# Accumulator loads moved to the front of each product, with their buffers swapped, and one GpSimd instruction taken off the root of a norm

## The chip, the cores and the metric

The kernel runs on one core of a Trainium2 chip. The metric is the device time of one execution in microseconds (us); lower is better. Most executions of one kernel agree within 0.3%.

## What is computed

The reference is one hybrid decoder block on x of 1024 rows by 1024 columns, in float32. Only its second half is touched here:

```python
x = x + jnp.einsum('bse,ed->bsd', mix, w_out[l])          # mix: retention and attention heads
h2 = rms_norm(x, norm2_g[l])
ff = jax.nn.silu(jnp.einsum('bsd,df->bsf', h2, w_gate[l])) * jnp.einsum('bsd,df->bsf', h2, w_up[l])
x = x + jnp.einsum('bsf,fd->bsd', ff, w_down[l])
```

`rms_norm` divides each row by the root of its mean square plus 1e-6. The hidden width D_FF is 2816.

## The kernel before

Every float32 product is made of three matmuls on rounded parts (`mm3`): each operand is split into a high part (a cast on ScalarE, tiles `whi` or the first half of `act`) and a low part (a subtraction on VectorE, tiles `wlo` or the second half of `act`). The three matmuls are high by high, high by low, low by high, so the second one needs the low part of the right operand.

The rows are eight tiles t of 128. The columns are two halves of 512, q or dh. Two stages matter.

**The middle stage** (`mid`, with `MID_PLAN`) computes `x2 = x + mix @ w_out` tile by tile on TensorE, and beside it the second norm. The plan is a list of (step, operation, arguments), and the engines keep its order. For a tile t: `o_add` adds x (VectorE) and stores the half to DRAM as `x2d`; `n_square` squares a half on ScalarE and sums each row into a column of the small tile `sso`; `n_rs` (lines 1024 to 1029) turns the two sums into the inverse root on GpSimd, with three instructions: add the two columns, times 1/D plus EPS, power of -0.5; `n_scale` multiplies each half of x2 by that root and the gain on VectorE, in place; `n_turn` transposes it on TensorE into a PSUM bank `h`; `n_back`, `n_hi`, `n_lo`, `f_sum` and so on make the operands of a Strassen product out of it. GpSimd also holds the first weight sums of the gate (`gw_sum`, tile `sum` from `rawp`).

**The gate and up stage** computes the hidden activations in eleven column groups of 256. In each, the four gate results are tiles of the pool `rowb`, the four up results tiles of the pool `rowa` (both named `c`; each pool has eight buffers), and VectorE multiplies up by gate. The results, and five sums of them (`plane`, tile `fsum`, made on GpSimd), are stored to DRAM as `ffd`.

**The last stage** multiplies by w_down, as seven Strassen products n of eleven steps c each (lines 1294 to 1320). In step c the left operand is loaded from `ffd` into a ring of eight slots (`a_load`, eight steps ahead), the right operand comes from w_down (`w_get`) and is where needed summed on GpSimd (`sum` from `wide`); both are split (`operand`); then twelve matmuls of 128x512 follow. At the end of a product the four PSUM banks are added on VectorE into `acc` tiles. There are sixteen of these; each begins as a piece of `x2d`, loaded by a DMA at line 1311, and the pieces that the first three products need are listed in `STARTS`. The last column group's five `fsum` planes are made inside the first product, at the steps of `LAST`.

All of these loads and stores are issued from one queue, that of SyncE (SP), which takes them in order: one that waits holds back all behind it. A scheduler sets the final order on the queue and on GpSimd.

Of the kernel before, what the change touches and what calls it, by code (L numbers as in the profile page):

```python
# [10 lines left out]
F32 = mybir.dt.float32  # L11
F32R = mybir.dt.float32r
AF = mybir.ActivationFunctionType
ALU = mybir.AluOpType
AX = mybir.AxisListType

P = 128
S = 1024
D = 1024
# [7 lines left out]
EPS = 1e-6  # L27
# [306 lines left out]
def block_kernel(ctx: ExitStack, tc: tile.TileContext, x, norm1_g, w_in, ret_norm_g, dq_g, dk_g,  # L334
# [17 lines left out]
    V, A, G, T = Pinned(nc.vector), Pinned(nc.scalar), Pinned(nc.gpsimd), Pinned(nc.tensor)  # L352
# [7 lines left out]
    rowa = ctx.enter_context(tc.tile_pool(name="rowa", bufs=NT))  # L360
# [15 lines left out]
    def bankp():  # L376
        return psum.tile([P, 512], F32, tag="pp", name="pp")

    def mm3(o, ah, al, bh, bl, first, last):
        T.matmul(o, ah, bh, start=first, stop=False)  # L380
        T.matmul(o, ah, bl, start=False, stop=False)
        T.matmul(o, al, bh, start=False, stop=last)

    def rsqrt(dst, src, n):

        G.tensor_tensor(out=dst, in0=src, in1=nhalf[:, :n], op=ALU.pow)

    def bankm(shape):
        return psum.tile(shape, F32, tag="m", name="m")
# [499 lines left out]
    x2 = [[None, None] for _ in range(NT)]  # L889
# [58 lines left out]
    for s in range(ND + NR + 3):  # L948
# [13 lines left out]
        if s == ND + 3:  # L962
            dif.close()
            rowb = ctx.enter_context(tc.tile_pool(name="rowb", bufs=NT))
# [11 lines left out]
        t = s - ND - NR  # L976
# [14 lines left out]
    NH = NF // 2  # L991
# [4 lines left out]
    def bankh():  # L996
        return hps.tile([P, 512], F32, tag="h", name="h")
# [17 lines left out]
    sums = {}  # L1015

    def n_square(t, i):

        if t not in sums:
            sums[t] = st.tile([P, 2], F32, name="sso", bufs=4)  # L1020
        sq = ap.tile([P, 512], F32, tag="sq", name="sq", bufs=1)
        A.activation(sq, x2[t][i], AF.Square, accum_out=sums[t][:, i:i + 1])

    def n_rs(t):

        ss2 = sums[t]
        G.tensor_tensor(out=ss2[:, 0:1], in0=ss2[:, 0:1], in1=ss2[:, 1:2], op=ALU.add)
        G.tensor_scalar(ss2[:, 1:2], ss2[:, 0:1], 1.0 / D, EPS, op0=ALU.mult, op1=ALU.add)
        rsqrt(ss2[:, 0:1], ss2[:, 1:2], 1)

    def n_scale(t, q):
        h2[t] = x2[t]
# [178 lines left out]
    for at, f, *args in MID_PLAN:  # L1211
        if at > step:
# [4 lines left out]
    DOWN = [(((1, 1), None, None), ((1, 0), (0, 0), ALU.subtract), {(0, 0): 1, (1, 0): 1}, ()),  # L1217
            (((1, 0), (1, 1), ALU.add), ((0, 0), None, None), {(1, 0): 1, (1, 1): -1}, ((1, 0),)),
            (((1, 0), (0, 0), ALU.subtract), ((0, 1), (0, 0), ALU.add), {(1, 1): 1}, ()),
            (((0, 0), (1, 1), ALU.add), ((1, 1), (0, 0), ALU.add), {(0, 0): 1, (1, 1): 1}, ()),  # L1220
            (((0, 0), (0, 1), ALU.add), ((1, 1), None, None), {(0, 0): -1, (0, 1): 1}, ()),
            (((0, 0), None, None), ((0, 1), (1, 1), ALU.subtract), {(0, 1): 1, (1, 1): 1}, ((0, 1), (1, 1))),
            (((0, 1), (1, 1), ALU.subtract), ((1, 0), (1, 1), ALU.add), {(0, 0): 1}, ((0, 0),))]
# [12 lines left out]
    acc = [[None, None] for _ in range(NT)]  # L1236
    at = {}

    def w_get(c, j, dh):

        if (c, j, dh) not in at:
            f = 2 * c + j
            to = at[c, j, dh] = kept[len(at)]
            nc.sync.dma_start(to, w_down[0, f * P:(f + 1) * P, dh * 512:(dh + 1) * 512])
        return at[c, j, dh]

    def a_load(i):

        nc.sync.dma_start(ring[i % len(ring)], ffd[i // NH, i % NH])

    def plane(n, c):
        a0, a1, aop = DOWN[n][0]
        src = up[a0[1], a0[0]]
        if a1 is not None:
            both = ap.tile([P, 512], F32, tag="sum", name="fsum", bufs=2)
            G.tensor_tensor(out=both, in0=src, in1=up[a1[1], a1[0]], op=aop)
            src = both
        nc.sync.dma_start(ffd[n, c], src)
# [23 lines left out]
    def operand(x_, y_=None, op=None):  # L1282
        hi, lo = (wp.tile([P, 512], F32R, tag=tag_, name=tag_) for tag_ in ("whi", "wlo"))
        if y_ is not None:
            both = wp.tile([P, 512], F32, tag="raw", name="sum", bufs=NRAW)
            G.tensor_tensor(out=both, in0=x_, in1=y_, op=op)
            x_ = both
        A.copy(hi, x_)
        V.tensor_tensor(out=lo, in0=x_, in1=hi.bitcast(F32), op=ALU.subtract)
        return hi, lo  # L1290

    STARTS = [((0, 0), (1, 0)), ((1, 1),), ((0, 1),)]
    LAST = {3 + i: n for i, n in enumerate(n for n in range(7) if DOWN[n][0][1] is not None)}
    for n, (_, (b0, b1, bop), outs, done) in enumerate(DOWN):
        m = [bankh() for _ in range(4)] if n % 2 == 0 else [bankp(), bankp(), bankm([P, 512]), bankm([P, 512])]
        for c in range(NH):
            b = [w_get(c, *name) for name in (b0, b1) if name is not None]
            i = n * NH + c
            ah, al = operand(ring[i % len(ring)])
            if i + len(ring) < 7 * NH:  # L1300
                a_load(i + len(ring))
            bh, bl = operand(*b, bop) if bop else operand(*b)
            if i in LAST:
                plane(LAST[i], NH - 1)

            if n < len(STARTS) and c >= NH - 4:
                t0 = c - NH + 4
                for sh, dh in STARTS[n]:
                    t = 4 * sh + t0
                    acc[t][dh] = (rowb if dh else rowa).tile([P, 512], F32, tag="rowb" if dh else "rowa", name="acc")  # L1310
                    nc.sync.dma_start(acc[t][dh], x2d[t * P:(t + 1) * P, dh * 512:(dh + 1) * 512])
            for t in range(4):
                mm3(m[t], ah[:, t * P:(t + 1) * P], al[:, t * P:(t + 1) * P], bh, bl, c == 0, c == NH - 1)
        for t in range(4):
            for (sh, dh), sign in outs.items():
                o = acc[4 * sh + t][dh]
                V.tensor_tensor(out=o, in0=o, in1=m[t], op=ALU.add if sign > 0 else ALU.subtract)
                if (sh, dh) in done:
                    row = (4 * sh + t) * P
                    nc.sync.dma_start(out[0, row:row + P, dh * 512:(dh + 1) * 512], o)  # L1320
# [25 lines left out]
```

## Time and profile before

| | |
|---|---|
| median of 3 runs | 1228.01 us (1226.68 to 1230.36) |
| the profiled execution | 1226.93 us, of which the span from first to last instruction is 1225.1 us |
| TensorE busy | 1204.8 us (98%) |
| VectorE, GpSimd, ScalarE busy | 838.1, 570.8, 537.2 us |
| middle stage, TensorE | about 500 to 609 us from the span's start |
| last stage, TensorE | 1007 to 1219 us |
| granted TensorE clock, mean | 0.996 |

Rows of the timeline read: start, duration (both us), engine, line, operation, output and inputs, and how many instructions are merged; in brackets how long the engine sat idle before, and what ended that. PE is TensorE, DVE VectorE, ACT ScalarE, POOL GpSimd. Nearly all rows have line 347, that of a helper which issues every instruction, so that groups are told apart by tile names.

### The profile page before, as it was taken

Reading aid. Unit: us, or ns where it says so; the run is one execution under the profiler, and the core shown is the slowest. Engines: PE = TensorE matmul, PEld = TensorE weight load, DVE = VectorE, ACT = ScalarE, POOL = GpSimd, SP = SyncE. Lnnn points to the kernel's source line nnn. Section 1 sums busy time; section 2 is a strip of 40 time slices with the busy share of each in tenths; the row PEclk is TensorE's granted clock in tenths of the full one; section 3 lists DMA queues with packets and bytes.
Section 4 is the critical chain, followed back from the end, with each engine's and each line's share of the span. In section 5 each row is a group of like instructions: output and inputs, shape, how many; then the busy total and the mean of one; then the engine's idle time right before and its main releaser. Section 6 shows DMA issues by size and latency. Waiting matters only on the chain. (4 is left out here: it accounts for less than half of the span.)

```text
span 1225.1 us, 17316 instructions
## 1 busy us (share of the span) xinstructions
PE 1204.8 (98%) x5944; PEld 1020.6 (83%) x5944; DVE 838.1 (68%) x1491; ACT 537.2 (44%) x1194; POOL 570.8 (47%) x719
## 2 busy tenths in 40 slices
PE   8999999999999999999899999999999999999998
PEld 7898989888888888787688888888888888788887
DVE  6988888854444445545997665757657659698697
ACT  6856666643222224434544344333443434344442
POOL 2656555644444443102276456545566536154053
PEclk9999999999999999999999999999999999999999
DMA  6201011102111111422233333323334177943342
GB/s 201 67 21 32 27 30 35 44 17 88 52 35 40 39 35 45 154 84 72 60 122 119 95 103 112 128 71 103 104 112 129 69 254 247 349 144 99 95 116 83
DMA packets 97383, 117.34 MB, mean 96 GB/s; under 512 B 8976, under 2 KB 60304, under 8 KB 97296
## 3 DMA queue, kind: packets, MB, share of 16 engines
q1 hardware_dynamic: 95968, 115.65, 29.5%
q8 instruction: 47, 0.77, 0.3%
q10 hardware_dynamic: 1328, 0.60, 0.3%
q14 instruction: 40, 0.33, 0.1%
HBM read 87.64 MB, written 28.57 MB: 95 GB/s over the span
## 5 line engine op out<-in xcount | busy, mean ns | idle before, releaser
L347 PE MATMUL pp<-whi,act 128*128 128x384 f32 (+1 forms) x896 | 287.8, 373 | 0.7 <-ACT whi L347 0.7
L347 POOL TENSOR_TENSOR sum<-rawp 128x512 f32<-128x512 f32 x110 | 157.2, 1430 | 174.5 <-DVE wlo L347 152.6
L347 ACT CAST whi<-sum 128x512 fp32r<-128x512 f32 x165 | 102.6, 622 | 204.9 <-PE h L347 62.8
L347 DVE TENSOR_TENSOR wlo<-sum,whi 128x512 fp32r<-128x512 f32 x165 | 167.7, 1016 | 34.0 <-ACT whi L347 33.5
L347 PE MATMUL h<-act,whi 128*128 128x512 f32 x608 | 187.5, 389 | 0.3 <-DVE act L347 0.3
L347 PEld LDWEIGHTS pp<-whi,act 128*128 128x128 f32 x896 | 167.4, 189 | 15.2 <-ACT whi L347 1.0
L347 PE MATMUL pp<-wlo,act 128*128 128x384 f32 (+1 forms) x448 | 161.6, 361 | 0.6 <-DVE wlo L347 0.6
L347 POOL TENSOR_TENSOR sum<-wide 128x512 f32<-128x512 f32 x55 | 85.7, 1560 | 134.0 <-DVE wlo L347 101.9
L347 PEld LDWEIGHTS h<-act,whi 128*128 128x128 f32 x608 | 114.1, 188 | 24.5 <-DVE act L347 0.7
L347 PE MATMUL pp<-wrh,act 128*128 128x512 f32 x384 | 130.7, 402 | 0.0
L347 PE MATMUL h<-act,wlo 128*128 128x512 f32 x304 | 118.3, 389 | 0.0
L347 DVE TENSOR_TENSOR wlo<-wide,whi 128x512 fp32r<-128x512 f32 x99 | 78.5, 816 | 32.5 <-ACT whi L347 32.5
L347 PE MATMUL m<-act,whi 128*128 128x512 f32 x312 | 97.7, 394 | 1.8 <-ACT act L347 1.2
L347 ACT CAST whi<-wide 128x512 fp32r<-128x512 f32 x99 | 59.3, 620 | 87.3 <-PE m L347 48.0
L347 PE MATMUL pp<-act,whi 128*128 128x512 f32 x312 | 96.4, 390 | 0.7 <-DVE act L347 0.7
L347 PEld LDWEIGHTS pp<-wlo,act 128*128 128x128 f32 x448 | 85.1, 190 | 7.6 <-DVE wlo L347 1.2
L347 POOL TENSOR_TENSOR fsum<-c 128x512 f32<-128x512 f32 x55 | 79.2, 1451 | 11.0 <-DMA ffd<-fsum 11.0
L347 PEld LDWEIGHTS pp<-wrh,act 128*128 128x128 f32 x384 | 72.2, 188 | 14.3
L347 DVE TENSOR_TENSOR c<-c,h 128x512 f32<-128x512 f32 x88 | 58.1, 682 | 32.6 <-PE h L347 32.5
L347 DVE TENSOR_TENSOR wlo<-rawp,whi 128x512 fp32r<-128x512 f32 x44 | 47.4, 1077 | 41.1 <-ACT whi L347 40.2
L347 PE MATMUL pp<-wrl,act 128*128 128x512 f32 x192 | 74.8, 390 | 0.0
L347 PEld LDWEIGHTS m<-act,whi 128*128 128x128 f32 x312 | 59.2, 190 | 14.6 <-ACT act L347 1.4
(162 smaller groups left out, 2515.7 us busy)
## 6 DMA issues: line engine op xcount, KB each, us to landing
wide<-ffd SPq DMA_DIRECT2D x77, 256.0 KB, 2.7
ffd<-fsum SPq DMA_DIRECT2D x55, 256.0 KB, 2.0
rawp<-in_w_gate_dram SPq DMA_DIRECT2D x22, 512.0 KB, 3.8
rawp<-in_w_up_dram SPq DMA_DIRECT2D x22, 512.0 KB, 3.9
wide<-in_w_down_dram SPq DMA_DIRECT2D x44, 256.0 KB, 5.3
raw<-in_w_in_dram SPq DMA_DIRECT2D x32, 256.0 KB, 2.8
ffd<-c SPq DMA_DIRECT2D x22, 256.0 KB, 2.0
raw<-in_w_in_dram SPq DMA_DIRECT2D x26, 192.0 KB, 2.5
```

Of the source, the lines that this page charges most:

```text
L347: i = getattr(self.engine, op)(*args, **kw)
```

## The change

The root: ScalarE's square now scales its input by D to the power of -0.5, so that the sums come out as means. After a tile's first square, a GpSimd instruction adds EPS to that column at once. `n_rs` then has two instructions, the add of the columns and the power. So there are still three per tile, but one of them stands earlier.

The accumulators: a product n of the first three loads its `acc` pieces at its steps 0 to 3 and no longer at steps 7 to 10, and the pieces with dh = 0 now lie in `rowb`, those with dh = 1 in `rowa`. The steps of `LAST` move from 3 to 7 to 4 to 8.

```diff
-        A.activation(sq, x2[t][i], AF.Square, accum_out=sums[t][:, i:i + 1])
+        A.activation(sq, x2[t][i], AF.Square, scale=D ** -0.5, accum_out=sums[t][:, i:i + 1])
+
+        if t not in eased:
+            eased.add(t)
+            G.tensor_scalar(sums[t][:, i:i + 1], sums[t][:, i:i + 1], EPS, None, op0=ALU.add)
+
+    eased = set()
...
         G.tensor_tensor(out=ss2[:, 0:1], in0=ss2[:, 0:1], in1=ss2[:, 1:2], op=ALU.add)
-        G.tensor_scalar(ss2[:, 1:2], ss2[:, 0:1], 1.0 / D, EPS, op0=ALU.mult, op1=ALU.add)
-        rsqrt(ss2[:, 0:1], ss2[:, 1:2], 1)
+        rsqrt(ss2[:, 0:1], ss2[:, 0:1], 1)
...
-    LAST = {3 + i: n for i, n in enumerate(n for n in range(7) if DOWN[n][0][1] is not None)}
+    LAST = {4 + i: n for i, n in enumerate(n for n in range(7) if DOWN[n][0][1] is not None)}
...
-            if n < len(STARTS) and c >= NH - 4:
-                t0 = c - NH + 4
+            if n < len(STARTS) and c < 4:
                 for sh, dh in STARTS[n]:
-                    t = 4 * sh + t0
-                    acc[t][dh] = (rowb if dh else rowa).tile([P, 512], F32, tag="rowb" if dh else "rowa", name="acc")
+                    t = 4 * sh + c
+                    acc[t][dh] = (rowa if dh else rowb).tile([P, 512], F32, tag="rowa" if dh else "rowb", name="acc")
                     nc.sync.dma_start(acc[t][dh], x2d[t * P:(t + 1) * P, dh * 512:(dh + 1) * 512])
```

The order on TensorE, VectorE and ScalarE is the same as before. On SP's queue, these rows follow the last of the loads of w_down for the first product (`ffd<-c` and `ffd<-fsum` are stores of the last column group, `wide<-ffd` are ring loads). Before:

```order
L1258 DMA ffd<-c 128x512 x2
L1249 DMA wide<-ffd 128x512 x4
L1258 DMA ffd<-fsum 128x512
L1249 DMA wide<-ffd 128x512
L1258 DMA ffd<-fsum 128x512
L1249 DMA wide<-ffd 128x512
L1258 DMA ffd<-fsum 128x512
L1249 DMA wide<-ffd 128x512
L1258 DMA ffd<-fsum 128x512
L1249 DMA wide<-ffd 128x512
L1258 DMA ffd<-fsum 128x512
L1311 DMA acc<-x2d 128x512 x2
```

At the same place after the change (its lines stand four or five further down in the file):

```order
L1263 DMA ffd<-c 128x512 x2
L1254 DMA wide<-ffd 128x512 x3
L1315 DMA acc<-x2d 128x512 x2
L1254 DMA wide<-ffd 128x512
L1315 DMA acc<-x2d 128x512 x2
L1254 DMA wide<-ffd 128x512
L1263 DMA ffd<-fsum 128x512
L1254 DMA wide<-ffd 128x512
L1263 DMA ffd<-fsum 128x512
L1254 DMA wide<-ffd 128x512
L1263 DMA ffd<-fsum 128x512
L1254 DMA wide<-ffd 128x512
```

Before, the eight pieces for the first product's sums begin behind the fifth store of an `fsum`. Now the first four of them go out in the gate and up stage's last group (where four pieces for the second product stood), and the other four stand here, ahead of the first store of an `fsum`. The pieces for the second and third product now follow behind the fifth store.

On GpSimd, around the roots of tiles 5, 6 and 7 (`sso_6756`, `sso_6850`, `sso_6953`), with the gate's weight sums between them. Before:

```order
L347 TENSOR_TENSOR sso_6756<-sso_6756 128x1
L347 TENSOR_SCALAR sso_6756<-sso_6756 128x1
L347 TENSOR_TENSOR sso_6756<-sso_6756,cs_77 128x1
L347 TENSOR_TENSOR sum_6880<-rawp_6405,rawp_6407 128x512
L347 TENSOR_TENSOR sso_6850<-sso_6850 128x1
L347 TENSOR_SCALAR sso_6850<-sso_6850 128x1
L347 TENSOR_TENSOR sso_6850<-sso_6850,cs_77 128x1
L347 TENSOR_TENSOR sum_6932<-rawp_6405,rawp_6407 128x512
```

After:

```order
L347 TENSOR_TENSOR sso_6756<-sso_6756 128x1
L347 TENSOR_TENSOR sso_6756<-sso_6756,cs_77 128x1
L347 TENSOR_SCALAR sso_6850<-sso_6850 128x1
L347 TENSOR_TENSOR sum_6881<-rawp_6408,rawp_6410 128x512
L347 TENSOR_TENSOR sso_6850<-sso_6850 128x1
L347 TENSOR_TENSOR sso_6850<-sso_6850,cs_77 128x1
L347 TENSOR_TENSOR sum_6932<-rawp_6408,rawp_6410 128x512
L347 TENSOR_SCALAR sso_6953<-sso_6953 128x1
```

The instruction between add and power is gone, and the one that adds EPS for tile 6 now stands ahead of the gate's first weight sum, where it waits for the first square of tile 6. That of tile 7 stands behind the second weight sum.

## Prediction

> **What bounds the kernel now.** I read the page first, then the waits of TensorE, then the timelines where it waited.
>
> ```profile
> span 1225.1 us, 17316 instructions
> ```
>
> The execution took 1226.93 us, so 1.8 us lie around this span. It is 1.08 us below the median of the runs, 1228.01; the sum is made against the execution and then moved up by that. TensorE is busy 98% of the span, so only time in which it stands still, or runs slowly, can be won. Stretches of the span by engine show where (busy us and instructions of PE, PEld, DVE, ACT, POOL, then granted clock, DMA share, GB/s):
>
> ```profile
> 505.00:605.00 100.00, 94.08 (x432) 75.65 (x431) 62.03 (x87) 42.54 (x86) 18.53 (x31) 0.98 0.28 92
> ...
> 1037.00:1067.00 30.00, 27.11 (x113) 21.94 (x112) 19.05 (x28) 10.99 (x20) 4.42 (x3) 0.94 0.98 345
> ```
>
> TensorE lacks 5.9 of 100 us in the one and 2.9 of 30 in the other, and the granted clock is below 1.00 in both. The change touches both: the roots lie in the first, the moved loads' sums in the second. Who made TensorE wait (total us, times, longest):
>
> ```profile
> PE pp L347 <- DVE wlo L347: 4.0, 4, 2.9
> PE h L347 <- DVE x L347: 3.2, 4, 1.2
> ```
>
> The longest single wait is 2.9 us for a low part `wlo`. TensorE there, at the beginning of the second product's third step:
>
> ```profile
> 1042.38 0.39 PE L347 MATMUL pp<-whi 128*128 128x512 f32 x1
> 1045.65 0.50 PE L347 MATMUL pp<-wlo,whi 128*128 128x512 f32 x1 [2.89 <-DVE wlo L347]
> ...
> 1047.55 0.63 PE L347 MATMUL m<-whi,wlo 128*128 128x512 f32 x1
> 1047.98 0.63 PE L347 MATMUL m<-whi 128*128 128x512 f32 x1
> ...
> 1050.54 0.42 PE L347 MATMUL pp<-whi 128*128 128x512 f32 x1
> ...
> 1051.03 0.39 PE L347 MATMUL pp<-whi,wlo 128*128 128x512 f32 x1
> ```
>
> And the chain that ended last gives the full pace, six matmuls in 1.36 us, 0.227 each:
>
> ```profile
> 1052.78 1.36 PE pp L347 x6
> ```
>
> From 1042.38 to 1051.03 there are 17 matmuls: 8.65 us where full pace takes 3.85. So 4.80 us are lost: 1045.65 - 1042.38 - 0.23 = 3.04 standing still, and 1.76 because from about 1047.2 to 1050.5 the starts lie 0.43 apart, half pace. The half pace begins 1.5 us behind the stop and ends by itself after 3.4; I count it with the stop.
>
> VectorE at the same time explains the stop:
>
> ```profile
> 1032.89 3.09 DVE L347 TENSOR_TENSOR wlo<-wide,whi 128x512 fp32r<-128x512 f32 x5
> 1036.41 0.69 DVE L347 TENSOR_TENSOR acc<-acc,h 128x512 f32<-128x512 f32 x1 [0.44 <-PE h L347]
> 1037.71 0.69 DVE L347 TENSOR_TENSOR acc<-acc,h 128x512 f32<-128x512 f32 x1 [0.61 <-DMA acc<-x2d]
> ...
> 1043.71 1.28 DVE L347 TENSOR_TENSOR acc<-acc,h 128x512 f32<-128x512 f32 x2 [0.69 <-DMA acc<-x2d]
> 1044.91 7.68 DVE L347 TENSOR_TENSOR wlo<-wide,whi 128x512 fp32r<-128x512 f32 x9
> ```
>
> Five splits end at 1035.98. Then eight adds of the first product stand ahead of the split that TensorE wants. The last two adds start at 1043.71 and take 0.60 each until the next instruction; eight would take 4.8. But they take from 1036.41 to 1044.91, 8.5, because most of them wait for their piece of `x2d`. SP's queue says why the pieces are late:
>
> ```profile
> 1012.51 0.80 SPq L1258 DMA_DIRECT2D ffd<-c  x2
> 1013.41 4.05 SPq L1249 DMA_DIRECT2D wide<-ffd  x4
> ...
> 1032.82 0.92 SPq L1311 DMA_DIRECT2D acc<-x2d  x2
> ```
>
> ```profile
> DMA to landing us min/median/max: 2.0/3.5/6.8
> ```
>
> The first two leave at 1032.82, and landing takes 3.5 in the median, up to 6.8. (The first add's 0.44 is put down to TensorE; 1032.82 + 3.5 = 1036.3 says it was the load.)
>
> **Part 1: the accumulators' loads.** Four of the eight pieces now leave in the gate stage, the other four behind three ring loads that follow the `ffd<-c` stores of 1012.51. Their slots in `rowb` are the last gate tiles, which VectorE's multiplications free before that very store can leave. The four ring loads at 1013.41 took 4.05 with their waits, so I put the last of the pieces at about 1019 and, at the longest landing, in place by 1026, 10 us ahead of the first add. The adds then run from 1035.98 at 0.60 each to 1040.8. The split behind them needs 0.74 (1044.91 to TensorE's 1045.65), so it is there at 1041.5; TensorE asks at 1042.61. Margin 1.1. The whole 3.04 goes, and with the stop its 1.76: **4.80 us**.
>
> What is late next? On SP's queue, ring loads and `fsum` stores now stand behind four more pieces: about 2 us later at 1017, where the ring is eight steps of 2.7 (twelve matmuls) ahead of TensorE. Behind the fifth store, eight pieces for later sums are mixed with loads of w_down, which the third product needs, nine steps or 24 us after the stop; DMA is busy 0.98 of that stretch, but four loads fewer fall into it. On GpSimd the third `fsum` moves behind the last weight sum, and the fifth must wait for the third's store; the number of its instructions ahead of the adds is the same. If one or two of them fall beside VectorE's splits that ran alone before, each costs VectorE about 1.0 (a scaling below takes 1.77 beside a GpSimd sum and 0.75 alone): with one the margin is used up, with two about 1 us of the stop stays. Bounds: 3.8 to 4.8.
>
> **Part 2: the root.** TensorE waits for a scaled tile four times. Tile 0 waits for something else: its second scaling follows the store of that half, which must have been read out before it is overwritten.
>
> ```profile
> 510.70 0.75 DVE L347 SCALAR_TENSOR_TENSOR x<-x,sso,gtile 128x512 f32<-128x512 f32 x1 [2.07 <-DMA x2d<-x]
> ```
>
> That gives nothing. Tile 5:
>
> ```profile
> 556.26 0.19 POOL L347 TENSOR_TENSOR sso<-sso 128x1 f32<-128x1 f32 x1 [10.71 <-ACT sq L347]
> ...
> 556.54 0.19 POOL L347 TENSOR_SCALAR sso<-sso 128x1 f32<-128x1 f32 x1
> ...
> 556.82 0.54 POOL L347 TENSOR_TENSOR sso<-sso,cs 128x1 f32<-128x1 f32 x1
> ...
> 557.33 1.29 POOL L347 TENSOR_TENSOR sum<-rawp 128x512 f32<-128x512 f32 x1
> 557.40 2.43 DVE L347 SCALAR_TENSOR_TENSOR x<-x,sso,gtile 128x512 f32<-128x512 f32 x2 [1.37 <-POOL sso L347]
> ...
> 559.31 0.63 PE L347 MATMUL h<-cs,x 128*128 128x128 f32 x4 [0.59 <-DVE x L347]
> ```
>
> From one GpSimd instruction to the next are 0.28, so without the middle one the power ends 0.28 earlier. More happens behind it. The weight sum at 557.33 ran beside the first scaling, and the scalings differ by whether one does:
>
> ```profile
> L347 DVE SCALAR_TENSOR_TENSOR x<-x,sso,gtile x16: 739/749/1772, 507.9 to 585.8; 128x512 f32<-128x512 f32 x16
> ```
>
> The median is 0.75, the longest 1.77. Now the sum stands behind the EPS instruction of tile 6, which waits for that tile's first square:
>
> ```profile
> 563.67 0.19 ACT L347 ACTIVATION_READ_ACCUMULATOR sq<-x 128x1 f32 x1
> ...
> 568.67 0.60 ACT L347 CAST whi<-sum 128x512 fp32r<-128x512 f32 x1
> ...
> 570.44 1.77 DVE L347 SCALAR_TENSOR_TENSOR x<-x,sso,gtile 128x512 f32<-128x512 f32 x1 [0.44 <-POOL sso L347]
> ...
> 572.36 0.63 PE L347 MATMUL h<-cs,x 128*128 128x128 f32 x4 [0.38 <-DVE x L347]
> ```
>
> The square's sum is there at 563.9, so the weight sum runs at about 564.2 to 565.5, and its cast is not due before 568.67. The first scaling of tile 5 then takes 0.75: 1.0 + 0.28 earlier, more than the 0.59 that TensorE waits. I take **0.59**. By the start alone (0.28) the term would be 0.28. [...]
>
> Tile 6 (the last two rows): TensorE idles 0.38; the power starts 0.28 earlier, and the scaling, 1.77 here, may get ahead of the weight sum. I take **0.38** (0.2 to 0.38). Tile 7:
>
> ```profile
> 581.35 0.58 POOL L347 TENSOR_TENSOR sso<-sso 128x1 f32<-128x1 f32 x1 [0.63 <-ACT sq L347]
> ...
> 582.01 0.51 POOL L347 TENSOR_SCALAR sso<-sso 128x1 f32<-128x1 f32 x1
> ...
> 582.61 0.55 POOL L347 TENSOR_TENSOR sso<-sso,cs 128x1 f32<-128x1 f32 x1
> ...
> 583.20 0.75 DVE L347 SCALAR_TENSOR_TENSOR x<-x,sso,gtile 128x512 f32<-128x512 f32 x1 [0.72 <-POOL sso L347]
> ...
> 586.69 0.63 PE L347 MATMUL h<-cs,x 128*128 128x128 f32 x4 [1.06 <-DVE x L347]
> ...
> 589.61 0.68 PE L347 MATMUL m<-act,whi 128*128 128x512 f32 x1 [0.63 <-DVE act L347]
> ...
> 593.59 0.40 PE L347 MATMUL m<-act,wlo 128*128 128x512 f32 x1
> ```
>
> Here a small GpSimd instruction takes 0.60, and VectorE's scaling waits for it with 0.72 idle. The 0.60 pass on to the transposes at 586.69 (1.06 idle) and in part to the low part at 589.61, which has sums and splits between them: **0.5** (0.36 to 0.60). The EPS instructions add 0.28 each where GpSimd otherwise waits for the square; the square itself keeps its shape and gets a constant factor, for which I take 0. The largest they could cost is 8 x 0.28 = 2.2 if each stood on the path, and none does.
>
> From 589.61 to 593.59 TensorE starts ten matmuls: 3.98 us where full pace takes 2.27, again about half pace after a broken stretch. I leave this 1.71 in the likeliest case, since of the idle time there (1.06 and 0.63 in these rows, more between them) most stays. Sum of part 2: 0.59 + 0.38 + 0.5 = 1.5; bounds 0 to 2.0.
>
> **Sum.** 4.80 + 1.5 = 6.3 us. The profiled execution: 1226.93 - 6.3 = 1220.6; the median of runs: 1228.01 - 6.3 = **1221.7**.
>
> **The rivals.**
>
> *The second half-paced stretch goes too.* In the last stage half pace begins after one long stop, here after several short waits. If the shorter waits of tile 7 no longer suffice, another 1.71 is won: 1220.0. For: half of the 1.06 ahead of it goes. Against: the rest stays. [...]
>
> *Only the last stage wins.* VectorE's list at tiles 5 to 7 is dense, and what a root gives, the next operand takes. Part 2 gives 0: 1223.2.
>
> *The stop stays in part.* GpSimd's later `fsum` and early sums of the third product hold VectorE twice or three times: 1 to 2 us stand still, perhaps with half pace: 2 to 3.5 us less won, about 1225.
>
> *The moved loads do not help.* The order shows them moved, so this would need them to land after 1036 all the same: 1228.
>
> *Slower.* SP's queue stops at a moved piece. Place: the four pieces behind 1013.41, with ring loads and stores behind them. The first ring load behind them serves the second product's first step; TensorE comes there two steps ahead of 1042.38, at 1036.9, and a load needs 3.5 to land, 0.60 for a cast (the row at 568.67) and 0.74 for a split, so a hold until 1032 costs nothing. Beyond, TensorE stands still for as long, and loses 1.76 at half pace on top. To end 3.7 above before, after a gain of 6.3, the hold must last until 1040 (8.2 + 1.8 = 10). The slot is free at 1012.5, so I see nothing that holds it.
>
> **How the numbers follow.** About 0.3%, 3.7 us, is what a measurement of this kernel can tell from no change. Chances: the forecast 0.48 (1221.7, give or take 1.3 for the bounds), the second half-paced stretch gone 0.17 (1220.0), last stage only 0.13 (1223.2), stop in part 0.10 (1225), no help 0.08 (1228), slower 0.04. Faster than 1224.3: the first three and a quarter of the fourth, 0.80. Same: 0.16. Slower: 0.04. The range must leave out no more than 0.2: it goes from 1218.7 (the second case less the bounds) to 1225.3.
>
> **What would show it.** After, TensorE's waits hold no wait of over 1 us for `wlo`, the clock in the thirty us after the first product is 1.00, the eight adds of the first product take 4.8, and no add waits for `acc`. The roots show two instructions, tile 5's first scaling 0.75, and the waits for scaled tiles fall from 3.2 to 1.8 or less. I am wrong if a new wait for `wlo` or `whi` stands at the beginning of the second product, if SP's queue shows a long gap ahead of a piece, or if the middle stage keeps its length.

## The result, and the profile after

The changed kernel takes 1221.8 us (median of 5 runs, 1221.46 to 1222.80), the kernel before 1228.59 beside it (5 runs, 1226.68 to 1230.36). The ratio is 0.9946, with a 95% interval of 0.9933 to 0.9959: faster, by about half a per cent. The profiled execution took 1221.46 with a span of 1219.5; before's took 1226.93 with 1225.1.

The same stretches of the span as before (busy us and instructions of PE, PEld, DVE, ACT, POOL, then granted clock, DMA share, GB/s):

```profile
505.00:605.00 100.00, 94.73 (x436) 76.44 (x436) 62.16 (x89) 43.16 (x87) 18.57 (x28) 0.98 0.28 94
1037.00:1067.00 30.00, 30.00 (x134) 24.82 (x134) 20.84 (x33) 12.64 (x23) 5.76 (x4) 1.00 1.03 369
```

In the last stage TensorE is now busy all 30 us, at full clock; it was 27.11 at 0.94. In the middle stage it gained little: 94.73 against 94.08, clock 0.98 as before. Who makes TensorE wait (total us, times, longest):

```profile
PE h L347 <- DVE x L347: 2.4, 2, 1.5
...
PE pp L347 <- DVE wlo L347: 1.1, 3, 0.5
```

The wait of 2.9 for a low part is gone. Of the four waits for a scaled tile two are left, and one of these has grown, from 1.18 to 1.52. VectorE at the first product's end:

```profile
1031.14 4.19 DVE L347 TENSOR_TENSOR wlo<-wide,whi 128x512 fp32r<-128x512 f32 x5
1035.25 4.86 DVE L347 TENSOR_TENSOR acc<-acc,h 128x512 f32<-128x512 f32 x8
1040.03 4.29 DVE L347 TENSOR_TENSOR wlo<-wide,whi 128x512 fp32r<-128x512 f32 x7
```

One row holds all eight sums: 4.78 from its start to the next row's, where before they needed 8.50, and none waits for a piece. The pieces in SP's queue:

```profile
1011.84 0.80 SPq L1263 DMA_DIRECT2D ffd<-c  x2
...
1015.92 0.90 SPq L1315 DMA_DIRECT2D acc<-x2d  x2
...
1017.33 0.91 SPq L1315 DMA_DIRECT2D acc<-x2d  x2
```

The last four for the first product's sums leave by 1018.24, not from 1032.82 on.

Where the time came from can be read off instructions that both kernels have, at three places. Before (VectorE, SP, and TensorE's last matmul), and then after:

```profile
499.95 0.68 DVE L347 TENSOR_TENSOR x<-pp,xr 128x512 f32<-128x512 f32 x1
...
968.31 0.34 SPq L1258 DMA_DIRECT2D ffd<-c  x1
...
1221.03 0.39 PE L347 MATMUL h<-whi,wlo 128*128 128x512 f32 x1
```

```profile
500.05 0.68 DVE L347 TENSOR_TENSOR x<-pp,xr 128x512 f32<-128x512 f32 x1
...
967.42 0.34 SPq L1263 DMA_DIRECT2D ffd<-c  x1
...
1215.44 0.39 PE L347 MATMUL h<-whi,wlo 128*128 128x512 f32 x1
```

The changed kernel is 0.10 behind at 500 us, 0.89 ahead at 968 and 5.59 ahead at the end. So the middle stage won 0.99, and the last stage 4.70.

Every run of this study has these three places in its profile, one profiled execution for each run. What lies between them differs less from run to run than whole times do, because executions reach the first place at times that lie 2 us apart (499.84 to 501.87), whatever the edit. The table has the first stretch (from the first place to the second: the middle stage, and the gate and up stage behind it) and the last stage (from the second place to the third). In the first stretch one wait varies by chance, that of TensorE for tile 0's second scaling; a column takes it off. All in us; the runs are told in the next section.

| run | first stretch | tile 0's wait | without it | last stage |
|---|---|---|---|---|
| before | 468.36 | 1.18 | 467.18 | 252.72 |
| after | 467.37 | 1.52 | 465.85 | 248.02 |
| the root alone | 467.10 | 1.28 | 465.82 | 252.99 |
| the loads alone | 469.32 | 2.16 | 467.16 | 247.89 |
| early steps, no swap | 466.92 | 1.12 | 465.80 | 247.90 |
| swap, late steps | 469.39 | 2.01 | 467.38 | 249.13 |
| planes' sums earlier | 467.51 | 1.68 | 465.83 | 248.28 |
| extra sums, four pieces | 466.98 | 1.16 | 465.82 | 252.47 |
| extra sums, two pieces | 467.85 | 2.05 | 465.80 | 248.15 |
| six matmuls in the gap | 467.22 | 1.25 | 465.97 | 247.89 |
| weight sum first | 467.85 | 1.49 | 466.36 | 248.25 |
| gate loads late, not held | 467.29 | 1.50 | 465.79 | 248.20 |
| gate loads late, held | 465.62 | none | 465.62 | 248.37 |
| transposes later | 465.62 | none | 465.62 | 248.02 |

Two runs have the old root: 467.18 and 467.16 without tile 0's wait. Seven have the new root and nothing else changed that acts in the first stretch (after, root alone, no swap, planes' sums, both with extra sums, gate loads not held): 465.79 to 465.85. So the root is worth 1.35, and the 0.99 above is that less the 0.34 by which tile 0's wait happened to be longer. The last stage takes 247.9 to 248.4 wherever the pieces come early and nothing is added that stops TensorE.

### The profile page after: what moved, and what is told of

Its sections match the earlier page's. It is cut to its first block, busy times and chain, and to the rows that moved or that the text cites. A ratio compares the mean times of both kernels' runs of the same rounds, so it can differ in the third digit from the quotient of the medians.

```text
span 1219.5 us, 17318 instructions
## 1 busy us (share of the span) xinstructions
PE 1200.6 (98%) x5944; PEld 1016.9 (83%) x5944; DVE 834.0 (68%) x1491; ACT 537.5 (44%) x1194; POOL 571.6 (47%) x719
## 4 chain that ended last, share of the span: by engine, by line
PE 92%; DVE 4%; DMA 2%; ACT 1%; issue 1%; POOL 0%; ACTq 0%; DVEq 0%; POOLq 0%
PE pp L347 42%; PE h L347 26%; PE m L347 18%; PE big L347 3%; PE o L347 2%; PE it L347 1%; DVE act L347 1%; DMA raw<-in_w_in_dram 1%; DVE sum L347 1%; DMA x2d<-x 0%; DMA cs<-in_const_dram 0%; DVE wlo L347 0%; DMA p<-in_x_dram 0%; DVE x L347 0%; DVE q L347 0%
```

## The experiments

### The two halves of the change, one at a time

The root alone: the lines of the last stage are put back.

```diff
-    LAST = {4 + i: n for i, n in enumerate(...
+    LAST = {3 + i: n for i, n in enumerate(...
...
-            if n < len(STARTS) and c < 4:
+            if n < len(STARTS) and c >= NH - 4:
+                t0 = c - NH + 4
...
-                    t = 4 * sh + c
-                    acc[t][dh] = (rowa if dh else rowb).tile(...
+                    t = 4 * sh + t0
+                    acc[t][dh] = (rowb if dh else rowa).tile(...
```

> The kernel before with the two-instruction root alone; the last stage's loads stay as they were. Theory (two separate gains): 1227.5 us, about 1.0 below before's 1228.5, because the middle stage of the changed kernel was 1.0 ahead at 985 us and that lead is the root's; the stop of about 3 us ahead of a weight remainder near 1042 us and the half pace behind it are still there. Rival A (the root's lead is eaten later, since the last stage waits for transfers and not for TensorE): 1228.5, no difference. [...]

Measured: 1226.63 us (12 runs, 1224.40 to 1230.41) against 1227.81 for before; ratio 0.9989, interval 0.9977 to 1.0002. The stop stands in full. TensorE there:

```profile
1046.38 0.50 PE L347 MATMUL pp<-wlo,whi 128*128 128x512 f32 x1 [3.17 <-DVE wlo L347]
...
1047.44 0.63 PE L347 MATMUL pp<-wlo,whi 128*128 128x512 f32 x1
1047.87 0.63 PE L347 MATMUL pp<-whi,wlo 128*128 128x512 f32 x1
```

It waits 3.17, and the starts behind that lie 0.43 apart. So the root alone is worth 1.2 by the medians, with an interval that just reaches no change. The table is sharper: without tile 0's wait the first stretch is 1.36 shorter than before's. The last stage is 0.27 longer, as its stop is (3.17, before 2.89), so rival A is right for 0.27 at most, in one profile each.

The loads alone: the root is put back.

```diff
-        A.activation(sq, x2[t][i], AF.Square, scale=D ** -0.5, accum_out=sums[t][:, i:i + 1])
-        if t not in eased:
-            eased.add(t)
-            G.tensor_scalar(sums[t][:, i:i + 1], sums[t][:, i:i + 1], EPS, None, op0=ALU.add)
+        A.activation(sq, x2[t][i], AF.Square, accum_out=sums[t][:, i:i + 1])
...
-        rsqrt(ss2[:, 0:1], ss2[:, 0:1], 1)
+        G.tensor_scalar(ss2[:, 1:2], ss2[:, 0:1], 1.0 / D, EPS, op0=ALU.mult, op1=ALU.add)
+        rsqrt(ss2[:, 0:1], ss2[:, 1:2], 1)
```

> The changed kernel with the old three-instruction root; only the loads' move and the swapped places are left of the change. Theory (two separate gains): 1222.9 us, about 5.7 below before (4.8 by the sum of the prediction, 5.7 by the parts that the result shows), eight sums on VectorE in 4.8 to 4.9 us without a wait, clock 1.00 in the 30 us behind the first product; tile 5's first scaling long again (1.77). Rival (the last stage's gain needs the lead of the middle stage): 1225 or more, and some of the stop or the half pace is back.

Measured: 1223.07 us (7 runs, 1222.62 to 1225.36), ratio 0.9961, interval 0.9947 to 0.9975: 4.7 below before. The last stage takes 247.89, which is 4.83 less than before's (the changed kernel: 4.70). The eight sums:

```profile
1036.53 4.86 DVE L347 TENSOR_TENSOR acc<-acc,h 128x512 f32<-128x512 f32 x8
```

They run without a wait though the middle stage has no lead, so the rival falls: the loads' gain needs nothing of the root. Of the change's gain the loads make about four fifths (4.70 of the 5.69 that the profiles differ by).

### Step and place of the loads

The change moves the loads to earlier steps and swaps the tiles that they go into. First the early steps without the swap:

```diff
-                    acc[t][dh] = (rowa if dh else rowb).tile([P, 512], F32, tag="rowa" if dh else "rowb", name="acc")
+                    acc[t][dh] = (rowb if dh else rowa).tile([P, 512], F32, tag="rowb" if dh else "rowa", name="acc")
```

> The changed kernel with the loads at the first four steps, but into the places as before: the first product's eight pieces in the tiles that the up products' planes leave, not in those of the gate's. Five of the eight are issued as early as in the changed kernel, the last three behind the pieces of the last planes, so from about 1030 us. Theory (both halves are needed, but only the last pieces count): the last three land at 1033 to 1037, the sums need them at 1038 to 1041, so 0 to 1 us is lost: 1222.3. Rival A (the place decides: the loads wait for GpSimd's plane sums whatever step they are written at): half or more of the gain is lost, 1225 or more, and a wait of over 1 us for acc on VectorE. Rival B (only the step decides): 1221.8 and no wait at all.

Measured: 1222.33 us (7 runs, 1220.96 to 1223.11), ratio 0.9958, interval 0.9946 to 0.9970: not to be told from the changed kernel, and nor is the last stage (247.90 against 248.02). SP's queue, the fifth of the eight pieces and the last two, and VectorE's sums:

```profile
1015.82 0.41 SPq L1315 DMA_DIRECT2D acc<-x2d  x1
...
1032.42 0.80 SPq L1315 DMA_DIRECT2D acc<-x2d  x2
```

```profile
1034.67 4.86 DVE L347 TENSOR_TENSOR acc<-acc,h 128x512 f32<-128x512 f32 x8
```

Three pieces do leave late, as the theory had it, but they are the last that are added, and no sum waits for them: that is what rival B said. Rival A falls. Then the swap with the late steps:

```diff
-            if n < len(STARTS) and c < 4:
+            if n < len(STARTS) and c >= NH - 4:
...
-                    t = 4 * sh + c
+                    t = 4 * sh + c - NH + 4
```

> The changed kernel with the swapped places, but with the loads at the last four steps as before. Theory (the queue's order decides: they are issued among the ring's and the weights' loads from about 1030 us): acc lands as late as before for the last pieces, VectorE's eight sums wait and the stop at the first product's end is back in most of its size: 1225.0 us (1223.5 to 1227). Rival (the swap alone carries the gain since the tiles are free early): 1221.8, and no wait for acc.

Measured: 1222.40 us (10 runs, 1221.87 to 1225.84), ratio 0.9960, interval 0.9949 to 0.9971. The theory put 1225.0, and the stop came back in a small part only. The profiled execution is the longest of the ten, so its total is not read; what makes it long lies ahead of the last stage (the table, and the last section). VectorE and TensorE at the first product's end:

```profile
1038.70 2.47 DVE L347 TENSOR_TENSOR acc<-acc,h 128x512 f32<-128x512 f32 x4
1041.54 0.69 DVE L347 TENSOR_TENSOR acc<-acc,h 128x512 f32<-128x512 f32 x1 [0.38 <-DMA acc<-x2d]
```

```profile
1046.18 0.50 PE L347 MATMUL pp<-wlo,whi 128*128 128x512 f32 x1 [0.70 <-DVE wlo L347]
1046.52 0.39 PE L347 MATMUL pp<-whi,wlo 128*128 128x512 f32 x1
1046.75 0.40 PE L347 MATMUL pp<-whi 128*128 128x512 f32 x1
```

Four sums have their pieces in time, because the swap gives these pieces tiles that are free in the gate and up stage: four loads leave SP's queue from 981.50 on, and the other four from 1037.29. The sums of those wait, and TensorE waits 0.70 (0.86 is lost from start to start). Behind so short a stop it goes on at full pace (0.23 from start to start). So by the table the early steps alone bring all of the last stage's gain, and the swap alone 3.6 of the 4.70 (249.13 against 252.72). The loss was so large before because all eight pieces were late.

### The planes' sums one step earlier

```diff
-    LAST = {4 + i: n for i, n in enumerate(...
+    LAST = {3 + i: n for i, n in enumerate(...
```

> The changed kernel with the last planes' sums started at step 3, as before, not at step 4. Theory (this part of the change is worth nothing, since no ring piece is waited for): 1221.8 us, the first plane sum about 2 to 3 us earlier on GpSimd, no other wait. Rival (the plane sums compete with VectorE or delay the loads that follow them in the queue): 1222.5 to 1224, with a wait for acc or for a ring piece of over 0.5 us.

Measured: 1223.33 us, a single run, beside 1228.20 for before. The eight sums took 4.86 here too, and no wait for a piece stands in the last stage, so the rival's mechanism is not there. The last stage takes 248.28, and the other runs with early pieces and no added stop have 247.89 to 248.37: if the moved step is worth anything, it is less than these differ by. Most of the distance to 1221.8 lies ahead of the middle stage, which this execution reaches 1.59 later (501.64 against 500.05).

### Is the half pace the stop's doing?

The changed kernel with extra sums on VectorE behind the eight, which delay the split that TensorE wants, without any late transfer; four pieces, and then two:

```diff
+        for op in (ALU.subtract, ALU.add) if n == 0 else ():
+            for t in range(4):
+                V.tensor_tensor(out=acc[t][0], in0=acc[t][0], in1=m[t], op=op)
```

> The changed kernel with eight extra sums on VectorE behind the eight of the first product (four pieces are taken out of four accumulators and added again; the result changes by rounding only): the stop of before is made again without any late transfer. Eight extra sums of 0.60 are 4.8 us, less the margin of 1.1: TensorE stands still for about 3.6 us. Theory (the half pace behind the stop comes from the stop alone): 1.4 to 1.8 us of half pace follow, 5.2 lost in all, 1227.0 us. Rival (the half pace came with the transfers that crowded there, or by chance): full pace behind the stop, 1225.4.

Measured: 1227.99 us (10 runs, 1226.44 to 1228.96), ratio 0.9998, interval 0.9985 to 1.0010. By the medians the whole gain is gone; by the table the last stage lost 4.45 of its 4.70. VectorE and TensorE, and then the thirty us behind 1037:

```profile
1035.93 9.64 DVE L347 TENSOR_TENSOR acc<-acc,h 128x512 f32<-128x512 f32 x16
```

```profile
1046.37 0.80 PE L347 MATMUL pp<-wlo,whi 128*128 128x512 f32 x1 [2.75 <-DVE wlo L347]
...
1047.38 0.63 PE L347 MATMUL pp<-wlo,whi 128*128 128x512 f32 x1
1047.81 0.63 PE L347 MATMUL pp<-whi,wlo 128*128 128x512 f32 x1
```

```profile
1037.00:1067.00 30.00, 27.25 (x114) 22.11 (x113) 21.89 (x35) 11.15 (x20) 4.15 (x3) 0.94 1.02 349
```

A wait of 2.75, and the starts 0.43 apart behind it, with all pieces in place. So the stop brings the half pace without any late piece. The transfers are as dense as in the changed kernel (share 1.02, there 1.03), whose clock is 1.00: their crowd alone does not bring it. A stop without the crowd was not tried here.

> The same with four extra sums: 2.4 us less the margin of 1.1, so TensorE stands still for about 1.3 us. Theory (a short stop does not halve the pace; the run with late loads in swapped places had 0.86 of stop and kept full pace): 1223.1 us, clock 1.00 behind the stop. Rival (any stop of over 1 us does): 1.4 to 1.8 us of half pace, 1224.7. If there is no stop at all, the margin was over 2.4 us and not 1.1.

Measured: 1223.89 us (5 runs, 1222.34 to 1224.33), ratio 0.9963, interval 0.9950 to 0.9976. There was no stop to judge by: the scheduler put three more matmuls that need only the high part ahead of the late split, as it did in the run with four pieces. That bought 0.68, and the rest lay in the margin.

```profile
1036.88 7.25 DVE L347 TENSOR_TENSOR acc<-acc,h 128x512 f32<-128x512 f32 x12
```

Twelve sums take 7.18 to the next split, 2.40 more than eight, and TensorE loses 0.12 from start to start. So the margin that the prediction put at 1.1 was about 1.6 here (2.40 - 0.68 - 0.12), and 1.2 in the run with four pieces (4.78 longer sums, 0.68 bought, 2.91 lost from start to start). The experiment says nothing on short stops; the run with late loads, with 0.86, does.

### Does the other half-paced stretch cost what the prediction says?

Six matmuls are put into the idle time ahead of the middle stage's half-paced stretch:

```diff
             m = self.m[n] = next_bank()
+            if self.first and n == 1:
+                self.idle = hi, b
+            if self.first and n == 2:
+                for _ in range(6):
+                    T.matmul(m, self.idle[0][:, 0, :], self.idle[1][:, :, 0, 0, :], start=True, stop=True)
```

> The changed kernel with six extra matmuls of 128x512 ahead of the third gate product, on operands of the second and into a bank that the product then starts anew: they lie in the idle 1.16 us before 587.56. Theory (half pace follows a stretch in which TensorE was mostly idle): the half pace behind 589.3 goes, worth up to 1.7 us, less up to 0.3 that the extra matmuls delay the product: 1220.3 us against the changed kernel's 1221.8. Rival A (the idle still left in that stretch is enough for half pace): 1221.8 to 1222.1. Rival B (the half pace is not due to idleness): the same matmuls at half pace, 1221.8 to 1222.1, and no shorter half-paced stretch.

Measured: 1223.35 us (7 runs, 1221.11 to 1227.15), ratio 0.9964, interval 0.9947 to 0.9981: no gain over the changed kernel. Nor is there one in the first stretch (465.97 without tile 0's wait, the seven runs 465.79 to 465.85). The half pace left its place and came back behind the next two waits. The row has two matmuls, and the next begins 0.85 behind their start, where 0.46 is full pace:

```profile
594.48 1.05 PE L347 MATMUL pp<-act,whi 128*128 128x512 f32 x2
```

That it would not have paid anyway is shown by the run without the swap, whose edit touches the last stage alone. TensorE in the changed kernel, from the transposes of tile 7 to the first matmul of the fifth gate product, and then in the run without the swap:

```profile
585.77 0.63 PE L347 MATMUL h<-cs,x 128*128 128x128 f32 x4 [0.91 <-DVE x L347]
...
589.70 1.05 PE L347 MATMUL m<-act,whi 128*128 128x512 f32 x2
...
596.68 0.39 PE L347 MATMUL h<-act,whi 128*128 128x512 f32 x1
```

```profile
585.52 0.63 PE L347 MATMUL h<-cs,x 128*128 128x128 f32 x4 [0.91 <-DVE x L347]
...
592.65 0.51 PE L347 MATMUL pp<-act,whi 128*128 128x512 f32 x1 [1.43 <-ACT act L347]
...
596.42 0.39 PE L347 MATMUL h<-act,whi 128*128 128x512 f32 x1
```

The first has the half pace (two matmuls in 1.05), the second hasn't. Both take 10.9 us (10.91 and 10.90), and so does the kernel before, whose half-paced stretch is longer (10.92, from 586.69 to 597.61). Where the third product runs at full pace, TensorE waits 1.43 for the fourth product's operand, which ScalarE makes no earlier. So this half pace lies beside a wait and costs nothing.

### Where tile 5's gain comes from

One GpSimd instruction moved: the one that adds EPS for tile 6 stands behind the gate's first weight sum.

```diff
-    (89, "gw_sum", 0),
+    (89, "gw_sum", 0), (89, "n_ease", 6),
...
-        if t not in eased:
+        if t not in eased and t != 6:
...
+    def n_ease(t):
+        G.tensor_scalar(sums[t][:, 0:1], sums[t][:, 0:1], EPS, None, op0=ALU.add)
```

> The changed kernel with one GpSimd instruction moved: tile 6's scale-free eps instruction stands behind the first gate weight sum, not ahead of it, so that the sum starts where it did before the change. Theory (tile 5's gain of about 0.6 us came from the weight sum, which no longer runs beside the scaling): tile 5's first scaling is long again, 1.4 to 1.8 us instead of 0.74, TensorE waits 0.5 to 0.75 longer there, 1222.4 us. Rival (the gain came from the shorter root): the scaling may be long but TensorE waits under 0.2 longer, 1221.8.

Measured: 1222.39 us, a single run beside 1228.20 for before, as the theory had it, though a run alone can't carry 0.6. The table and the rows carry it: without tile 0's wait the first stretch is 0.54 longer than in the seven runs. GpSimd, VectorE's two scalings of tile 5, and TensorE's transposes:

```profile
557.75 1.29 POOL L347 TENSOR_TENSOR sum<-rawp 128x512 f32<-128x512 f32 x1
```

```profile
557.82 2.44 DVE L347 SCALAR_TENSOR_TENSOR x<-x,sso,gtile 128x512 f32<-128x512 f32 x2 [1.18 <-POOL sso L347]
```

```profile
559.74 0.63 PE L347 MATMUL h<-cs,x 128*128 128x128 f32 x4 [0.40 <-DVE x L347]
```

The same scalings and transposes in the changed kernel:

```profile
557.66 1.42 DVE L347 SCALAR_TENSOR_TENSOR x<-x,sso,gtile 128x512 f32<-128x512 f32 x2 [1.18 <-POOL sso L347]
```

```profile
559.02 0.60 PE L347 MATMUL h<-cs,x 128*128 128x128 f32 x4
```

The weight sum starts 0.07 ahead of the scalings again, they take 2.44 again and not 1.42, and TensorE waits 0.40 where it waited 0.59 before the change. In the changed kernel it waits for nothing there. So of tile 5's 0.59, 0.19 is the shorter root and 0.40 the weight sum that the moved instruction holds back.

### Tile 0's store

The prediction gave tile 0 nothing, since its second scaling waits for the store of that half of x2. What does the store wait for? The first gate weights' loads were written later:

```diff
-        if step == 8:
+        if step == 40:
```

> The changed kernel with the loads of the first gate weights issued at step 40 of the middle stage, not at step 8: they are needed at step 89. It asks what tile 0's second scaling waits for. Theory (the store of x2's first tile shares the DMA engines with the gate weights' loads): the store lands 1 to 2.5 us earlier, the wait of 1.52 us of TensorE before 511.95 goes to under 0.5, and the time to 1220.6 us. Rival (the store is slow by itself or behind other loads): the wait stays at 1.2 to 1.6, 1221.8.

Measured: 1222.69 us (6 runs, 1221.65 to 1223.80), ratio 0.9953, interval 0.9939 to 0.9968. But the kernel does not do what the edit says. SP's queue:

```profile
501.03 0.38 SPq L1113 DMA_DIRECT2D rawp<-in_w_gate_dram  x1
...
506.70 0.33 SPq L917 DMA_DIRECT2D x2d<-x  x1
```

SP's instructions aren't held in the order of the plan; the scheduler put the loads where they were. The run tells nothing. With the loads tied to their place:

```diff
-                nc.sync.dma_start(r.rearrange(...
+                load = nc.sync.dma_start(r.rearrange(...
...
+                if self.first:
+                    tc.keep_in_program_order(load)
...
-        if step == 8:
+        if step == 40:
```

> The run on late gate loads left the queue as it was (the two loads of the first gate weights still stood at 501.03 and 502.47, ahead of the store of x2's second half at 506.70), so its question is open. Here the two loads are tied to their place at step 40, behind five further stores of x2. Theory (the store shares the DMA engines with the megabyte of gate weights): TensorE's wait before tile 0's second transposes, 1.12 to 2.16 us in the runs so far, goes to under 0.5, and the time to 1220.5 us, 1.3 below the changed kernel. Rival (the store is slow by itself): the wait stays at 1.1 to 1.6, 1221.8.

Measured: 1220.85 us (5 runs, 1219.08 to 1221.67) against 1227.11 for before; ratio 0.9940, interval 0.9925 to 0.9954. The wait is gone, as the theory had it. VectorE's two scalings of tile 0, TensorE's second transposes, and the landing of the stores in that stretch:

```profile
509.28 1.42 DVE L347 SCALAR_TENSOR_TENSOR x<-x,sso,gtile 128x512 f32<-128x512 f32 x2 [1.90 <-DMA x2d<-x]
```

```profile
511.71 0.60 PE L347 MATMUL h<-cs,x 128*128 128x128 f32 x4
```

```profile
x2d<-x SPq DMA_DIRECT2D x3, 256.0 KB, 2.1
```

The stores land in 2.1 us in the median (5.1 in the changed kernel, over the same 500 to 515 us), the scalings follow each other, and TensorE waits for neither. (The 1.90 of idle time in the row is the root's: the power ends at 509.25, and the changed kernel has the same 1.90 ahead of its first scaling.) In both kernels the store leaves the queue 0.03 behind the add that makes its half (507.41 behind 507.38, and 505.96 behind 505.93), so what the loads lengthen is the transfer and not the wait in the queue. The other way to the same end leaves the store late and gives TensorE other work:

```diff
-    (14, "n_turn", 0, 1),
...
-    (15, "n_back", 0, 1),
-    (16, "f_sum", 3, 0),
+    (17, "n_turn", 0, 1),
     (17, "o_add", 1, 1),
-    (17, "f_hi", 3, 0),
+    (17, "n_back", 0, 1),
+    (18, "f_sum", 3, 0),
...
+    (18, "f_hi", 3, 0),
```

> The changed kernel with the transposes of tile 0's second half put three steps (nine matmuls, 2.04 us) later in TensorE's order, with what hangs on them (the copy back, the first sum and its split). Tile 0's wait for its store, 1.30 to 1.69 us of TensorE in the runs of the changed kernel, can't be made shorter by moving other loads; so matmuls of the projection are put into it. Theory (the store lands while TensorE works on): no wait for a scaled tile near 512 us, and 1.4 us less than the changed kernel: 1220.5 us, 8 below before. Rival (the later copy back holds up tile 1's square, root or split): a wait of 0.5 to 1.5 at tile 1's transposes near 518 us, 1221.5.

Measured: 1221.49 us (6 runs, 1219.73 to 1222.39), ratio 0.9949, interval 0.9936 to 0.9962. TensorE's second transposes of tile 0:

```profile
512.37 0.60 PE L347 MATMUL h<-cs,x 128*128 128x128 f32 x4
```

They wait for nothing, and tile 1's (516.94) don't either, so the rival falls. Both versions beat the kernel before. In the first stretch both also beat the changed kernel, with 465.62 against 467.37. The whole times are too few to show it: the medians differ from the changed kernel's by 0.3 and 0.9, and the profiled executions took 1219.78 (transposes later) and 1221.67 (loads held), the changed kernel's 1221.46.

## Why the prediction was right

**The stop.** Part 1 put 4.80 us on the late pieces: 3.04 of stop and 1.76 of half pace. The last stage won 4.70, and the loads alone 4.7. The steps hold: pieces gone by 1018.24 (forecast: about 1019) and landed 5.9 later at most (6.8), sums in 4.78 (4.8), no stop. One reading was off: 3.5 is the landing's median over all sixteen piece loads, and the eight late ones took 5.6; no term hangs on it. The run with extra sums shows the half pace to be the stop's own, which the prediction had only taken so. The collision that it feared came once: five splits in 4.19, not 3.09, but before the sums and not in them.

What the argument did not see is how much slack there was. It treated the eight pieces as one. All but three early would have done, and half of them early would have brought 3.6 of the 4.70.

**The root.** The prediction's sum was 1.5. By the table the root is worth 1.35; the middle stage won 0.99 because tile 0's wait, which the prediction had left as it is, was 0.34 longer. The sum is nearly right, but its parts are less so. By tiles:

- Tile 5: 0.59 forecast, and the whole wait of 0.59 is gone, for the reason given (the two scalings take 1.42, not 2.43).
- Tile 6: 0.38 forecast, and that wait is gone too, though 0.1 comes back as idle time at the tile's second transposes.
- Tile 7: 0.5 forecast; the wait before its transposes went from 1.06 to 0.91. This is the step that failed. "The 0.60 pass on" took it that two small GpSimd instructions would last as long each as three did. They did not. GpSimd and VectorE at tile 7, after:

```profile
580.58 0.69 POOL L347 TENSOR_TENSOR sso<-sso 128x1 f32<-128x1 f32 x1 [0.52 <-ACT sq L347]
581.35 0.89 POOL L347 TENSOR_TENSOR sso<-sso,cs 128x1 f32<-128x1 f32 x1
```

```profile
580.54 1.28 DVE L347 TENSOR_TENSOR sum<-x,x 128x512 f32<-128x512 f32 x2
582.28 0.75 DVE L347 SCALAR_TENSOR_TENSOR x<-x,sso,gtile 128x512 f32<-128x512 f32 x1 [0.46 <-POOL sso L347]
```

The add took 0.69, the power 0.89 (0.58 and 0.55 before), the one beside VectorE's two sums and the other partly so. From the first instruction to the scaling are 1.70, where the three took 1.85: 0.15 won, not 0.60. At tile 1, with VectorE idle beside them, the same two take 0.20 and 0.56; here the power ends 0.42 behind the second sum. The instruction that was dropped had run beside those sums too, so it looks as if the two that are left are stretched there in its place. That is an estimate from these durations; no run here takes the sums away to show it.

- Tile 0: nothing forecast; its wait went from 1.18 to 1.52. That is no work of the change: the same wait is 1.12 to 2.16 in the runs of this study in which the gate loads stand ahead of the store and the transposes where they were.

From start to start (from tile 1's transposes to the second ones of tile 5, from these to tile 6's, and to tile 7's) the three tiles are worth 0.78, 0.46 and 0.14, and tile 0 ahead of them -0.36; together 1.02, beside the 0.99. Tiles 5 and 6 brought 0.27 more than forecast and so made up for most of tile 7's 0.36, which is luck. The prediction took their worth from the brackets. The idle time there begins at the end of the matmul ahead, 0.39 behind its start, where at full pace the next one begins after 0.23: a wait costs 0.16 more than its bracket (tile 5's 0.59 is 0.75 from start to start). Part 1 had counted from start to start, and was right. Of the signs that the prediction named one did not come: the waits for scaled tiles fell to 2.4 and not to 1.8, as 1.52 of them is tile 0's.

**The sum.** Forecast for the profiled execution 1220.6, measured 1221.46. Of the 0.8 between them 0.36 is tile 0, and 0.1 each are the root (1.47 against 1.35), the last stage, the lag at 500 us, and the time outside the span (1.96, before 1.83). The median came to 1221.8 where 1221.7 was said, and that is closer than the working deserves: before's profiled execution lay 1.08 under its median, after's only 0.34 under its own. With the kernel before at 1228.59 beside it, the medians say a gain of 6.8 and the profiled executions 5.5; the forecast of 6.3 lies between.

**The rivals.** "The second half-paced stretch goes too" had a wrong price. It put 1.71 on that stretch; in the run without the swap the stretch was gone, and nothing was won. It lay beside a wait for ScalarE's operand that takes its place (1.43). It was also no matter of the waits being shorter, since that run's waits are the same. "Only the last stage wins" falls by the table: what the root gave is not taken by the next operand, but is there in all seven runs. The root's own runs could not say so by their times, whose interval reaches no change. "The stop stays in part", "the moved loads do not help" and "slower" showed no trace.

## What to carry to other kernels

A load that an engine needs late can still stop another engine, through what is queued behind the instruction that waits for it (here TensorE stood 2.89 us for a split behind VectorE's sums, which took 8.50 with their waits and 4.78 without); issue it as soon as its place is free, and ahead of the stores that wait for something else. Price a dropped instruction by the time from the event ahead of it to the one behind it, not by its own length; here the two that were left stretched, from 0.58 and 0.55 to 0.69 and 0.89. And count a slow stretch only if no wait stands behind it: what ran at half pace here, ahead of an operand that was late anyway, cost nothing (10.91 us with the half pace, 10.90 without). For a gain of 1 us in 1228, compare the stretch that the edit touches, between instructions that both kernels have, and take off a wait that varies by itself: that gave the root's 1.35 within 0.1, where the medians of 12 and 19 runs gave an interval that reaches no change.

## What the runs showed of the hardware

The half pace follows a stop, but not by its length alone. TensorE's waits of 2.89, 3.17 and 2.75 us (before, the root alone, extra sums) were followed by it, one of 0.70 was not. In between it went both ways, at the same transposes of tile 0. The run with late loads and swapped places, and then the run with the loads alone:

```profile
513.77 0.90 PE L347 MATMUL h<-cs,x 128*128 128x128 f32 x4 [2.01 <-DVE x L347]
...
515.32 1.05 PE L347 MATMUL pp<-wrh,act 128*128 128x512 f32 x2
```

```profile
512.35 0.66 PE L347 MATMUL h<-cs,x 128*128 128x128 f32 x4 [2.16 <-DVE x L347]
...
513.30 0.63 PE L347 MATMUL pp<-wrh,act 128*128 128x512 f32 x2
```

A wait of 2.01 was followed by half pace (two matmuls in 1.05), a longer one of 2.16 was not (0.63). It shows in the table as well: 467.38 without the wait in the one, where the seven runs with this root have 465.8. What decides it beside the length of the stop, no run here shows.

Stores of 256 KB with two weight loads of 512 KB each beside them, issued 4 to 6 us ahead of the store that is waited for, landed in 5.1 us in the median of three, and in 2.1 without these loads, in one profile each. A scaling that overwrites the half waits until the store has landed: in the changed kernel it begins at 511.14, after 2.56 of idle time that ends with the store, and 5.18 behind the store's start in the queue.
